# Another finish for the last row block: mean and deviation as six rows, the root taken from the variance, five stores

## The chip, the cores and the metric

The kernel runs on one core of a Trainium2 chip. The metric is the device time of one execution in microseconds. Times of whole executions come from unprofiled runs; the profile is of one more execution, with its own time. "Span" is the stretch from the first to the last recorded instruction or transfer of that execution, and all times of the timeline count from the start of the span.

## The reference

A decoder trunk of two layers on one sequence of 512 tokens with 2048 features, in float32. Layer 0 is differential attention, layer 1 forgetting attention over shared keys and values. Each layer ends in a residual sum and a layer norm; the last one is where the change lies:

```python
def layer_norm(x, g, b):
    xf = x.astype(jnp.float32)
    mu = jnp.mean(xf, axis=-1, keepdims=True)
    var = jnp.mean(jnp.square(xf - mu), axis=-1, keepdims=True)
    y = (xf - mu) * lax.rsqrt(var + EPS)
    return (y * g.astype(jnp.float32) + b.astype(jnp.float32)).astype(x.dtype)
...
        x = layer_norm(DN_ALPHA * x + gate[:, None] * y, ln_g[l], ln_b[l])
```

Here `y` is the output projection of the attention, a product of 512 x 2048 by 2048 x 2048.

## The kernel before, in words

All large products are made in a split form: each float32 operand is split into a rounded part `hi` (type float32r, which TensorE takes in one pass) and the rest `lo`, and three products are summed (`products`, lines 208 to 210). ScalarE makes `hi` (lines 108, 113), VectorE `lo` (lines 109, 114).

The last stage is `out_projection(oB, 1, ...)` (line 1188, called at 1784). It takes the 2048 output columns in four groups f of 512, and the 512 tokens in four row blocks b of 128 partitions. For f = 0, 1, 2 VectorE multiplies the product by the gate, adds the scaled residual, puts the sum into the tile `z` (128 partitions, 4 blocks, 2048 columns) and takes statistics of the 512 columns (line 1243). For f = 3 the accumulators in PSUM start out filled with the residual and the gate is multiplied into the weights beforehand (line 104), so that the sum is ready when the last product ends. In that group the blocks are finished one after the other: six of the eight weight pieces are kept on chip (`held`), TensorE runs all of them for block 0, then for block 1, and so on. When a block's last product is done, `evac` takes the statistics of its last 512 columns (line 1234) and calls `norm_b(b, acc)` (line 1727).

`norm_b` of blocks 0 to 2 aggregates the statistics into mean and variance (`mv`, line 1733), adds EPS (1735), takes the root on ScalarE (1736), centres and multiplies by the gain (`centre`, 1741), forms the reciprocal root with one refining step (`root`, 1744 to 1746), multiplies by it and adds the bias (`finish`, 1750) and stores two halves (1751). While VectorE does that, TensorE multiplies for the next block.

Block 3 has nothing behind it, so its norm is split between engines. For the first 768 columns the formula is written as rstd * (z*g - mean*g + sqrt(var+EPS)*b). The product z*g is put into two PSUM banks ahead of time by `fold_last` (line 1721), which block 2's `norm_b` calls. The rows g and b of these columns are loaded into the tiles `ends`, two rows each (1723, 1724). When mean and deviation are there, they stand side by side in `ms` (128 x 2, lines 1763 and 1766), are transposed by TensorE (1771) and copied to `rows` by ScalarE (1773), and a product of 2 rows by the 512 or 256 columns of `ends` adds the two missing terms onto each bank (1775). These are plain float32 products. ScalarE then multiplies each bank by rstd (1776) and stores it, one from SyncE's queue, one from its own (1777). VectorE does columns 768 to 2047 in the old way: the last 512 are centred straight out of PSUM before the reciprocal root (1764), 768 to 1535 behind it (1778), and both are finished and stored (1779, 1780). Six products on a constant tile (`warm`, 1769) keep TensorE busy between the last product and the transpose.

What sets the order: the program is traced in the order of the code, then a planner with a model of the engines gives every engine its instructions in an order of its own, the traced order counting as priority, and places the waits. An instruction whose inputs are ready early may so be put far ahead of its place in the code. `keep(...)` pins an instruction behind the one traced before it on its engine. Only the start of the kernel has orders written out by hand. Small tiles of 512 columns come from a pool of 16 buffers (`kpool`, through `ktile`), of which weight pieces, residual rows and gates take their share in the last stage. Eight PSUM banks are held as four `acc`, two `sc`, one `tr` and one `o`.

Of the kernel before, what the change touches and what calls it, by code (L numbers as in the profile page):

```python
# [10 lines left out]
F32 = mybir.dt.float32  # L11
F32R = mybir.dt.float32r
I32 = mybir.dt.int32
AF = mybir.ActivationFunctionType
ALU = mybir.AluOpType

P = 128
D = 2048
KT = D // P
T = 512  # L20
# [4 lines left out]
EPS = 1e-5  # L25
# [119 lines left out]
def tile_yoco(  # L145
# [23 lines left out]
    nc = tc.nc  # L169
    V, S, PE, G = nc.vector, nc.scalar, nc.tensor, nc.gpsimd  # L170
# [3 lines left out]
    out = out[0]  # L174
    a_w_in, a_w_out, b_w_in, b_w_out = a_w_in[0], a_w_out[0], b_w_in[0], b_w_out[0]

    const = ctx.enter_context(tc.tile_pool(name="const", bufs=1))
    hpool = ctx.enter_context(tc.tile_pool(name="hpool", bufs=32))
    kpool = ctx.enter_context(tc.tile_pool(name="kpool", bufs=16))
# [10 lines left out]
    def acc_bank(name="acc"):  # L190
        return ps.tile([P, 512], F32, name=name, tag="acc", bufs=4)

    def sc_bank(name="sc"):
        return ps.tile([P, 512], F32, name=name, tag="sc", bufs=2)

    def tr_bank(name="tr"):
        return ps.tile([P, 512], F32, name=name, tag="tr", bufs=1)
# [14 lines left out]
    def corner(sc, q, k):  # L212
# [6 lines left out]
    ident = const.tile([P, P], F32, name="ident")  # L219
    make_identity(nc, ident)  # L220
    ones = const.tile([P, P], F32, name="ones")
    G.memset(ones, 1.0)
    mask = const.tile([P, 512], F32, name="mask")
    G.memset(mask, 0.0)
    G.affine_select(
        out=mask[:, 384:], in_=mask[:, 384:], compare_op=ALU.is_ge, fill=NEG, base=0, pattern=[[-1, P]],
# [13 lines left out]
    pt = tr_bank()  # L240
# [7 lines left out]
    pt = tr_bank()  # L248
# [10 lines left out]
    rows = {}  # L259
# [227 lines left out]
    with tc.tile_pool(name="start", bufs=2, reuse_waits="tile") as sp, tc.manual_schedule(engines=MANUAL):  # L487
# [50 lines left out]
        mtile, xts, acc2, pms, pxs, tmps, split_h, bank = {}, {}, {}, {}, {}, {}, {}, {}  # L538
# [283 lines left out]
    for dst, src, col, bias, one in (  # L822
# [3 lines left out]
        n = len(one)  # L826
# [242 lines left out]
    raw = {}  # L1069

    def keep(key, acc):
        raw[key] = kpool.tile([P, T], F32, name="raw", tag="K")
        S.copy(raw[key], acc)
# [98 lines left out]
    def ktile(name):  # L1172
        return kpool.tile([P, T], F32, name=name, tag="K")
# [197 lines left out]
    npool, n, nstats = zp  # L1371
# [75 lines left out]
    acc = [acc_bank() for _ in range(TB)]  # L1447
# [184 lines left out]
    def attention_pair(p):  # L1632
        sa, ra, da, ta, na, va = attention_b(2 * p)
        sb, rb, db, tb, nb, vb = attention_b(2 * p + 1)
        if p == 7:

            return [
                None, None, sa[0], sa[1], ra[0], [sa[2], ra[1]], da[0], [sa[3], da[1]], [ra[2], ta[0]], [sb[0], ta[1]],
                [ra[3], da[2]], sb[1], [ta[2], da[3]], sb[2], ta[3], va[0], va[1], [nb[0], sb[3]], nb[1], nb[2], None, nb[3], None,
                vb[0], vb[1],  # L1640
            ]
        steps = [
            [], [], [sa[0]], [sa[1]], [ra[0]], [sa[2], ra[1]], [da[0]], [sa[3], da[1]], [ra[2]], [sb[0], ta[0]],
            [ra[3], da[2]], [sb[1], ta[1]], [rb[0], da[3]], [sb[2], ta[2]], [rb[1]], [sb[3], ta[3]],
            [va[0], rb[2]], [va[1]], [db[0], db[1], rb[3]], [db[2]], [tb[0], db[3]], [tb[1]], [tb[2]], [tb[3]], [vb[0]], [vb[1]],
        ]
        return [todo or None for todo in steps]
# [26 lines left out]
    lnrow = {}  # L1674
# [36 lines left out]
        return fn  # L1711

    ahead = {}

    def fold_last():


        pool, z, _ = zp2
        for k, (f0, f1) in enumerate(((0, 512), (512, 768))):
            bank = sc_bank()[:, 0 : f1 - f0]  # L1720
            V.tensor_tensor(bank, z[:, 3, f0:f1], lnrow["g"][:, f0:f1], op=ALU.mult)
            ends = ktile("ends")[0:2, 0 : f1 - f0]
            nc.sync.dma_start(ends[0:1, :], ln_g[1, f0:f1].rearrange("(o n) -> o n", o=1))
            nc.sync.dma_start(ends[1:2, :], ln_b[1, f0:f1].rearrange("(o n) -> o n", o=1))
            ahead[k] = bank, ends, slice(f0, f1)

    def norm_b(b, acc):


        pool, z, stats = zp2  # L1730
        mv = pool.tile([P, 2], F32, name="mv", tag="mv", bufs=4)
        keep = tc.keep_in_program_order
        keep(V.bn_aggr(mv, stats[:, b, :, :]))
        ve, nh, a, rstd = (pool.tile([P, 1], F32, name=k, tag=k, bufs=4) for k in ("lve", "lnh", "lna", "lrstd"))
        keep(V.tensor_scalar(ve, mv[:, 1:2], EPS, None, op0=ALU.add))
        S.activation(rstd, ve, AF.Sqrt)
        keep(V.tensor_scalar(nh, ve, -0.5, None, op0=ALU.mult))

        def centre(f0, f1, src):
            fs = slice(f0, f1)  # L1740
            keep(V.scalar_tensor_tensor(z[:, b, fs], src, mv[:, 0:1], lnrow["g"][:, fs], op0=ALU.subtract, op1=ALU.mult))

        def root():
            keep(V.reciprocal(rstd, rstd))
            keep(V.scalar_tensor_tensor(a, rstd, nh, rstd, op0=ALU.mult, op1=ALU.mult))
            keep(V.scalar_tensor_tensor(rstd, a, 1.5, rstd, op0=ALU.add, op1=ALU.mult))

        def finish(f0, f1):
            fs = slice(f0, f1)
            keep(V.scalar_tensor_tensor(z[:, b, fs], z[:, b, fs], rstd, lnrow["b"][:, fs], op0=ALU.mult, op1=ALU.add))  # L1750
            nc.sync.dma_start(out[b * P : (b + 1) * P, fs], z[:, b, fs])

        if b < 3:
            centre(0, 1536, z[:, b, 0:1536])
            centre(1536, 2048, acc)
            root()
            finish(0, 1024)
            finish(1024, 2048)
            if b == 2:
                fold_last()  # L1760
            return
        ms = pool.tile([P, 2], F32, name="ms", tag="ms")
        keep(V.tensor_scalar(ms[:, 0:1], mv[:, 0:1], -1.0, None, op0=ALU.mult))
        centre(1536, 2048, acc)
        root()
        keep(V.tensor_tensor(ms[:, 1:2], ve, rstd, op=ALU.mult))
        warm = acc_bank("warm")
        for _ in range(6):
            keep(PE.matmul(warm[:, 0:256], mask[:, 0:P], mask[:, 0:256], start=True, stop=True))
        pt = tr_bank()  # L1770
        keep(PE.transpose(pt[0:2, 0:P], ms, ident))
        rows = pool.tile([2, P], F32, name="rows", tag="rows")
        S.copy(rows, pt[0:2, 0:P])
        for (bank, ends, fs), queue in zip(ahead.values(), (nc.sync, nc.scalar)):
            PE.matmul(bank, rows, ends, start=False, stop=True, skip_group_check=True)
            S.activation(z[:, b, fs], bank, AF.Copy, scale=rstd)
            queue.dma_start(out[b * P : (b + 1) * P, fs], z[:, b, fs])
        centre(768, 1536, z[:, b, 768:1536])
        finish(768, 1536)
        finish(1536, 2048)  # L1780

    pieces.extend(attention_pair(7))
    pieces.append(lambda: split_ogb((14, 15)))
    out_projection(oB, 1, zp2, open_z, residual_b, norm_b)
    drain()

# [27 lines left out]
```

## Time and profile before

| what | us |
|---|---|
| median of 3 runs (lowest, highest) | 1928.12 (1927.77, 1928.47) |
| the profiled execution, its own time | 1927.76 |
| its span | 1925.9 |
| TensorE busy in the span | 1911.3 |
| end of the last product of the projection | 1915.81 |
| first store of block 3 issued | 1920.66 |
| last store of block 3 issued | 1921.62 |

A line of the timeline gives start, duration, engine (PE is TensorE, PEld its weight loads, DVE VectorE, ACT ScalarE, POOL GpSimd; SPq and ACTq are DMA issues of SyncE and ScalarE), line of the code, operation, the tiles out<-in with their shapes, and how many instructions it stands for. In square brackets stands how long the engine was idle before it and what ended the wait. A line of the windows gives a stretch of the span, its length, the busy time of each engine, the granted TensorE clock, the busy share of the 16 DMA engines and GB/s. A line of the groups gives busy us, the mean duration of one in ns, and the idle time before.

### The profile page before, as it was taken

What the parts mean: (1) busy time and instruction counts of PE and PEld (TensorE: products, weight loads), DVE (VectorE), ACT (ScalarE), POOL (GpSimd) and SP (SyncE); (2) the same over time, 40 slices, a digit from 0 to 9 for tenths busy, and PEclk for the clock granted to TensorE, in tenths of its full rate; (3) what the DMA queues carried; (4) which work ended last, traced back from release to release, by engine and by line L of the source; (5) the groups of instructions that cost most, each with busy time, mean ns of one, the idle gap of its engine ahead of it and who ended that gap; (6) DMA issues with size and microseconds to landing.
All of it is one profiled execution on the core that took longest, in us unless ns stands there. A gap on an engine that the chain in (4) does not pass through costs nothing.

```text
span 1925.9 us, 25859 instructions
## 1 busy us (share of the span) xinstructions
PE 1911.3 (99%) x8924; PEld 1593.4 (83%) x8924; DVE 1369.5 (71%) x2611; ACT 731.3 (38%) x1262; POOL 2.2 (0%) x10
## 2 busy tenths in 40 slices
PE   8999999999999999999999999999999999999998
PEld 6888888888888888888888898888888888888887
DVE  7994588777676868667675477787566666686767
ACT  3656344333332344521272232224344444453121
POOL 0000000000000000000000000000000000000000
PEclk9999999999999999999999999999999999999999
DMA  9993566676767676476547586785355555555622
GB/s 341 385 336 91 160 186 196 209 239 191 233 199 226 204 222 182 122 241 216 187 165 255 180 296 208 247 272 160 114 150 154 161 150 158 154 153 175 222 90 110
DMA packets 352103, 382.20 MB, mean 198 GB/s; under 512 B 77882, under 2 KB 256082, under 8 KB 351204
## 3 DMA queue, kind: packets, MB, share of 16 engines
q1 hardware_dynamic: 348948, 376.23, 62.1%
q10 hardware_dynamic: 3024, 4.33, 0.6%
q8 instruction: 70, 1.15, 0.2%
q14 instruction: 61, 0.50, 0.1%
HBM read 348.65 MB, written 31.80 MB: 198 GB/s over the span
## 4 chain that ended last, share of the span: by engine, by line
PE 96%; DVE 2%; DMA 1%; SPq 1%; issue 0%; ACT 0%; DVEq 0%; ACTq 0%
PE acc L208 26%; PE acc L209 26%; PE acc L210 26%; PE acc L720 4%; PE sc L720 2%; PE sc L210 1%; PE sc L209 1%; PE sc L208 1%; PE o L208 1%; PE o L210 1%; PE o L209 1%; PE o L720 1%; DMA sms<-in_w_mod_dram 0%; SPq L568 0%; PE tr L686 0%
## 5 line engine op out<-in xcount | busy, mean ns | idle before, releaser
L113 ACT CAST whi<-wst 128x1024 fp32r<-128x1024 f32 (+2 forms) x298 | 303.3, 1018 | 616.4 <-PE acc L210 323.5
L114 DVE TENSOR_TENSOR wlo<-wst,whi 128x1024 fp32r<-128x1024 f32 (+2 forms) x298 | 351.6, 1180 | 241.2 <-ACT whi L113 221.4
L208 PE MATMUL acc<-hh,whi 128*128 128x512 f32 x1184 | 462.9, 391 | 0.0
L209 PE MATMUL acc<-hl,whi 128*128 128x512 f32 x1184 | 461.6, 390 | 0.0
L210 PE MATMUL acc<-hh,wlo 128*128 128x512 f32 x1184 | 460.1, 390 | 0.0
L208 PE MATMUL acc<-whi,hh 128*128 128x512 f32 (+1 forms) x1104 | 418.5, 379 | 0.0
L209 PE MATMUL acc<-wlo,hh 128*128 128x512 f32 (+1 forms) x1104 | 416.7, 377 | 0.0
L210 PE MATMUL acc<-whi,hl 128*128 128x512 f32 (+1 forms) x1104 | 416.2, 377 | 0.0
L433 DVE SCALAR_TENSOR_TENSOR macc<-ms,cact,macc 128x512 f32<-128x512 f32 x307 | 229.3, 747 | 69.9 <-DMA ms<-in_w_mod_dram 51.6
L210 PEld LDWEIGHTS acc<-hh,wlo 128*128 128x128 f32 x1184 | 222.3, 188 | 47.5
L208 PEld LDWEIGHTS acc<-hh,whi 128*128 128x128 f32 x1184 | 222.4, 188 | 44.0 <-DVE sgb L1509 0.8
L209 PEld LDWEIGHTS acc<-hl,whi 128*128 128x128 f32 x1184 | 222.5, 188 | 42.3
L210 PEld LDWEIGHTS acc<-whi,hl 128*128 128x128 f32 x1104 | 207.2, 188 | 38.7
L208 PEld LDWEIGHTS acc<-whi,hh 128*128 128x128 f32 x1104 | 207.3, 188 | 37.4 <-DVE ztmp L1241 0.6
L209 PEld LDWEIGHTS acc<-wlo,hh 128*128 128x128 f32 x1104 | 207.4, 188 | 36.0
L618 DVE SCALAR_TENSOR_TENSOR sacc<-sms,cact,sacc 128x512 f32<-128x512 f32 (+1 forms) x128 | 89.9, 703 | 6.2 <-DMA sms<-in_w_mod_dram 2.8
L904 ACT ACTIVATE e<-e,mn 128x128 f32<-128x128 f32 (+3 forms) x64 | 36.0, 563 | 109.1 <-DVE mn L900 102.5
L1559 ACT ACTIVATE eb<-eb,mnb 128x128 f32<-128x128 f32 (+1 forms) x64 | 35.9, 561 | 72.9 <-DVE mnb L1556 72.5
L720 PE MATMUL acc<-wlo,hh 128*128 128x512 f32 x128 | 49.9, 399 | 0.6 <-DVE wlo L132 0.6
L720 PE MATMUL acc<-whi,hl 128*128 128x512 f32 x128 | 49.4, 393 | 0.0
L720 PE MATMUL acc<-whi,hh 128*128 128x512 f32 x128 | 49.2, 393 | 0.0
L132 DVE TENSOR_TENSOR wlo<-wst,whi 128x768 fp32r<-128x768 f32 (+1 forms) x32 | 34.8, 1088 | 16.9 <-ACT whi L125 12.4
(321 smaller groups left out, 2093.9 us busy)
## 6 DMA issues: line engine op xcount, KB each, us to landing
wst<-in_a_w_in_dram SPq DMA_DIRECT2D x240, 256.0 KB, 3.9
ms<-in_w_mod_dram SPq DMA_DIRECT2D x136, 256.0 KB, 3.9
ms<-in_kv_w_mod_dram SPq DMA_DIRECT2D x64, 512.0 KB, 4.6
wst<-in_b_w_in_dram SPq DMA_DIRECT2D x128, 256.0 KB, 3.0
sms<-in_w_mod_dram SPq DMA_DIRECT2D x56, 512.0 KB, 7.4
wst<-in_kv_w_dram SPq DMA_DIRECT2D x56, 512.0 KB, 4.3
ms<-in_w_mod_dram SPq DMA_DIRECT2D x32, 512.0 KB, 5.1
wst<-in_a_w_out_dram SPq DMA_DIRECT2D x32, 512.0 KB, 4.7
```

Source lines behind the costliest of these rows:

```text
L113: self.nc.scalar.copy(hi[:, :, :w], st[:, :, :w])
L114: self.nc.vector.tensor_tensor(lo[:, :, :w], st[:, :, :w], hi[:, :, :w].bitcast(F32), op=ALU.subtract)
L132: self.nc.vector.tensor_tensor(lo[:, :, :w], st[:, :, :w], hi[:, :, :w].bitcast(F32), op=ALU.subtract)
L208: PE.matmul(dst, lhs[0], rhs[0], start=start, stop=False, skip_group_check=True)
L209: PE.matmul(dst, lhs[0], rhs[1], start=False, stop=False, skip_group_check=True)
L210: PE.matmul(dst, lhs[1], rhs[0], start=False, stop=stop, skip_group_check=True)
L433: ins = V.scalar_tensor_tensor(acc, w, cact[:, kt : kt + 1], acc, op0=ALU.mult, op1=ALU.add)
L618: V.scalar_tensor_tensor(acc, w, sc, acc, op0=ALU.mult, op1=ALU.add)
L720: PE.matmul(bank[n, bk], l, r, start=start, stop=stop, skip_group_check=True)
L904: S.activation(e[:, :w], e[:, :w], AF.Exp, bias=mn, scale=-1.0, accum_out=rs)
L1559: S.activation(e[:, :w], e[:, :w], AF.Exp, bias=mn, scale=-1.0, accum_out=rs)
```

## The change

Only block 3's norm, its preparation and one constant are changed.

The columns that go through PSUM grow from 768 to 1280, in three chunks of 512, 512 and 256; the third takes a bank of `acc`. They are prepared by the call for block 1 instead of block 2. Mean and deviation are each split into a rounded part and a rest, and g and b as well: the product has 6 rows (high mean and deviation with the high and the low parts of g and b, low mean and deviation with the high parts) and float32r operands. For that `ends_of` loads g and b into three pairs of rows, copies them on ScalarE (which rounds) and subtracts on VectorE to leave the low part in the first pair.

The root of block 3 is half the deviation, taken by ScalarE from the variance itself, with scale 0.25 and a constant tile `qeps` (0.25 * EPS, filled by GpSimd at the start) as bias. The deviation comes from it by one step of Newton, ahead of the reciprocal root, which gets its own step afterwards. The last 512 columns are centred behind the transpose. Five warming products are left of six. VectorE keeps columns 1280 to 2047. The five stores of the block are pinned in the order: chunk 0, columns 1536 to 2047, chunk 1 (all SyncE), chunk 2 (ScalarE's queue), columns 1280 to 1535 (SyncE).

```diff
--- before.py
+++ after.py
@@ -220,6 +220,8 @@
     make_identity(nc, ident)
     ones = const.tile([P, P], F32, name="ones")
     G.memset(ones, 1.0)
+    qeps = const.tile([P, 1], F32, name="qeps")
+    G.memset(qeps, 0.25 * EPS)
     mask = const.tile([P, 512], F32, name="mask")
     G.memset(mask, 0.0)
     G.affine_select(
@@ -1711,18 +1713,27 @@
         return fn
 
     ahead = {}
-
-    def fold_last():
-
-
+    CHUNKS = ((0, 512), (512, 1024), (1024, 1280))
+
+    def ends_of(f0, f1):
+
+
+        w = f1 - f0
+        raw = ktile("raw")[0:6, 0:w]
+        for k, src in enumerate((ln_g, ln_b)):
+            nc.sync.dma_start(raw[k:6:2, :], src[1, f0:f1].partition_broadcast(3))
+        ends = kpool.tile([P, T], F32R, name="ends", tag="K")[0:6, 0:w]
+        S.copy(ends, raw)
+        V.tensor_tensor(ends[0:2, :], raw[0:2, :], ends[0:2, :].bitcast(F32), op=ALU.subtract)
+        return ends
+
+    def fold_last(banks):
         pool, z, _ = zp2
-        for k, (f0, f1) in enumerate(((0, 512), (512, 768))):
-            bank = sc_bank()[:, 0 : f1 - f0]
-            V.tensor_tensor(bank, z[:, 3, f0:f1], lnrow["g"][:, f0:f1], op=ALU.mult)
-            ends = ktile("ends")[0:2, 0 : f1 - f0]
-            nc.sync.dma_start(ends[0:1, :], ln_g[1, f0:f1].rearrange("(o n) -> o n", o=1))
-            nc.sync.dma_start(ends[1:2, :], ln_b[1, f0:f1].rearrange("(o n) -> o n", o=1))
-            ahead[k] = bank, ends, slice(f0, f1)
+        for k, bank in banks:
+            fs = slice(*CHUNKS[k])
+            bank = bank()[:, 0 : fs.stop - fs.start]
+            V.tensor_tensor(bank, z[:, 3, fs], lnrow["g"][:, fs], op=ALU.mult)
+            ahead[k] = bank, ends_of(*CHUNKS[k]), fs
 
     def norm_b(b, acc):
 
@@ -1732,52 +1743,69 @@
         keep = tc.keep_in_program_order
         keep(V.bn_aggr(mv, stats[:, b, :, :]))
         ve, nh, a, rstd = (pool.tile([P, 1], F32, name=k, tag=k, bufs=4) for k in ("lve", "lnh", "lna", "lrstd"))
-        keep(V.tensor_scalar(ve, mv[:, 1:2], EPS, None, op0=ALU.add))
-        S.activation(rstd, ve, AF.Sqrt)
-        keep(V.tensor_scalar(nh, ve, -0.5, None, op0=ALU.mult))
 
         def centre(f0, f1, src):
             fs = slice(f0, f1)
             keep(V.scalar_tensor_tensor(z[:, b, fs], src, mv[:, 0:1], lnrow["g"][:, fs], op0=ALU.subtract, op1=ALU.mult))
 
-        def root():
+        def finish(f0, f1):
+            fs = slice(f0, f1)
+            keep(V.scalar_tensor_tensor(z[:, b, fs], z[:, b, fs], rstd, lnrow["b"][:, fs], op0=ALU.mult, op1=ALU.add))
+            store = nc.sync.dma_start(out[b * P : (b + 1) * P, fs], z[:, b, fs])
+            if b == 3:
+                keep(store)
+
+        if b < 3:
+            keep(V.tensor_scalar(ve, mv[:, 1:2], EPS, None, op0=ALU.add))
+            S.activation(rstd, ve, AF.Sqrt)
+            keep(V.tensor_scalar(nh, ve, -0.5, None, op0=ALU.mult))
+            centre(0, 1536, z[:, b, 0:1536])
+            centre(1536, 2048, acc)
             keep(V.reciprocal(rstd, rstd))
             keep(V.scalar_tensor_tensor(a, rstd, nh, rstd, op0=ALU.mult, op1=ALU.mult))
             keep(V.scalar_tensor_tensor(rstd, a, 1.5, rstd, op0=ALU.add, op1=ALU.mult))
-
-        def finish(f0, f1):
-            fs = slice(f0, f1)
-            keep(V.scalar_tensor_tensor(z[:, b, fs], z[:, b, fs], rstd, lnrow["b"][:, fs], op0=ALU.mult, op1=ALU.add))
-            nc.sync.dma_start(out[b * P : (b + 1) * P, fs], z[:, b, fs])
-
-        if b < 3:
-            centre(0, 1536, z[:, b, 0:1536])
-            centre(1536, 2048, acc)
-            root()
             finish(0, 1024)
             finish(1024, 2048)
-            if b == 2:
-                fold_last()
+            if b == 1:
+                fold_last(((0, sc_bank), (1, sc_bank), (2, acc_bank)))
             return
-        ms = pool.tile([P, 2], F32, name="ms", tag="ms")
-        keep(V.tensor_scalar(ms[:, 0:1], mv[:, 0:1], -1.0, None, op0=ALU.mult))
-        centre(1536, 2048, acc)
-        root()
-        keep(V.tensor_tensor(ms[:, 1:2], ve, rstd, op=ALU.mult))
+
+
+        half, inv = (pool.tile([P, 1], F32, name=k, tag=k) for k in ("half", "inv"))
+        S.activation(half, mv[:, 1:2], AF.Sqrt, scale=0.25, bias=qeps)
+        ms = pool.tile([P, 1, 2], F32, name="ms", tag="ms")
+        keep(V.tensor_scalar(ve, mv[:, 1:2], EPS, 0.25, op0=ALU.add, op1=ALU.mult))
+        keep(V.tensor_scalar(ms[:, 0, 0:1], mv[:, 0:1], -1.0, None, op0=ALU.mult))
+        keep(V.reciprocal(inv, half))
+        keep(V.scalar_tensor_tensor(ms[:, 0, 1:2], inv, ve, half, op0=ALU.mult, op1=ALU.add))
+        six = pool.tile([P, 3, 2], F32R, name="six", tag="six")
+        keep(V.tensor_copy(six[:, 0:2, :], ms.to_broadcast([P, 2, 2])))
+        keep(V.tensor_tensor(six[:, 2:3, :], ms, six[:, 0:1, :].bitcast(F32), op=ALU.subtract))
+        keep(V.tensor_scalar(nh, ve, -0.25, None, op0=ALU.mult))
+        keep(V.scalar_tensor_tensor(a, inv, nh, inv, op0=ALU.mult, op1=ALU.mult))
+        keep(V.scalar_tensor_tensor(rstd, a, 0.75, inv, op0=ALU.add, op1=ALU.mult))
         warm = acc_bank("warm")
-        for _ in range(6):
+        for _ in range(5):
             keep(PE.matmul(warm[:, 0:256], mask[:, 0:P], mask[:, 0:256], start=True, stop=True))
         pt = tr_bank()
-        keep(PE.transpose(pt[0:2, 0:P], ms, ident))
-        rows = pool.tile([2, P], F32, name="rows", tag="rows")
-        S.copy(rows, pt[0:2, 0:P])
-        for (bank, ends, fs), queue in zip(ahead.values(), (nc.sync, nc.scalar)):
+        keep(PE.transpose(pt[0:6, 0:P], six.bitcast(F32).rearrange("p u k -> p (u k)"), ident))
+        rows = pool.tile([6, P], F32R, name="rows", tag="rows")
+        S.copy(rows, pt[0:6, 0:P])
+        for bank, ends, _ in ahead.values():
             PE.matmul(bank, rows, ends, start=False, stop=True, skip_group_check=True)
-            S.activation(z[:, b, fs], bank, AF.Copy, scale=rstd)
-            queue.dma_start(out[b * P : (b + 1) * P, fs], z[:, b, fs])
-        centre(768, 1536, z[:, b, 768:1536])
-        finish(768, 1536)
+
+        def scaled(k, queue):
+            bank, _, fs = ahead[k]
+            keep(S.activation(z[:, b, fs], bank, AF.Copy, scale=rstd))
+            keep(queue.dma_start(out[b * P : (b + 1) * P, fs], z[:, b, fs]))
+
+        scaled(0, nc.sync)
+        centre(1536, 2048, acc)
         finish(1536, 2048)
+        scaled(1, nc.sync)
+        scaled(2, nc.scalar)
+        centre(1280, 1536, z[:, b, 1280:1536])
+        finish(1280, 1536)
 
     pieces.extend(attention_pair(7))
     pieces.append(lambda: split_ogb((14, 15)))
```

## The prediction

> **What bounds the kernel now.** I read the busy shares and the chain that ended last on the page first, then the timeline of the last 11 us, because the change touches little before them.
>
> ```profile
> PE 1911.3 (99%) x8924; PEld 1593.4 (83%) x8924; DVE 1369.5 (71%) x2611; ACT 731.3 (38%) x1262; POOL 2.2 (0%) x10
> PE 96%; DVE 2%; DMA 1%; SPq 1%; issue 0%; ACT 0%; DVEq 0%; ACTq 0%
> ```
>
> TensorE is busy for 99% of the span and is 96% of the chain. The matrix products are not touched, so the change can win only in what follows the last of them. That tail, in order of time (start, duration, engine, line):
>
> ```profile
> 1915.64 2.75 PE L1769 MATMUL warm<-mask 128*128 128x256 f32 x12
> 1915.85 0.70 DVE L1234 BATCH_NORM_STATS2 zstats<-acc 128x6 f32<-128x512 f32 x1 [1.36 <-PE acc L210]
> 1916.58 0.27 DVE L1733 BATCH_NORM_AGGREGATE mv<-zstats 128x2 f32<-128x24 f32 x1
> 1916.88 0.15 DVE L1735 TENSOR_SCALAR lve<-mv 128x1 f32<-128x1 f32 x1
> 1917.07 0.20 ACT L1736 ACTIVATE lrstd<-lve 128x1 f32<-128x1 f32 x1 [7.96 <-DVE lve L1735]
> ...
> 1917.86 0.15 DVE L1744 RECIPROCAL lrstd<-lrstd 128x1 f32<-128x1 f32 x1
> 1918.05 0.22 DVE L1745 SCALAR_TENSOR_TENSOR lna<-lrstd,lnh 128x1 f32<-128x1 f32 x1
> 1918.30 0.16 DVE L1746 SCALAR_TENSOR_TENSOR lrstd<-lna,lrstd 128x1 f32<-128x1 f32 x1
> 1918.49 0.16 DVE L1766 TENSOR_TENSOR ms<-lve,lrstd 128x1 f32<-128x1 f32 x1
> 1918.57 1.01 DVE L1741 SCALAR_TENSOR_TENSOR z<-z,mv,ln_g 128x768 f32<-128x768 f32 x1
> ...
> 1918.71 0.27 PE L1771 MATMUL tr<-ident,ms 128*2 128x128 f32 x1 [0.31 <-DVE ms L1766]
> 1919.02 0.26 ACT L1773 COPY rows<-tr 2x128 f32<-2x128 f32 x1 [1.75 <-PE tr L1771]
> ...
> 1919.33 1.55 PE L1775 MATMUL sc<-ends,rows 2*128 2x512 f32 x4 [0.34 <-ACT rows L1773]
> 1919.62 1.68 DVE L1750 SCALAR_TENSOR_TENSOR z<-z,lrstd,ln_b 128x768 f32<-128x768 f32 x2
> ```
>
> ```profile
> 1920.48 0.69 ACT L1776 ACTIVATE z<-sc,lrstd 128x512 f32<-128x512 f32 x1 [1.21 <-PE sc L1775]
> ```
>
> ```profile
> 1920.66 0.33 SPq L1751 DMA_DIRECT2D out_dram<-z  x1
> 1921.20 0.33 SPq L1777 DMA_DIRECT2D out_dram<-z  x1
> 1921.57 0.40 ACTq L1777 DMA_DIRECT2D out_dram<-z  x1
> 1921.62 0.41 SPq L1751 DMA_DIRECT2D out_dram<-z  x1
> ```
>
> Statistics, root, then two-row products on one side and elementwise work on the other; the first store is issued at 1920.66. After it the stretches of the span (the last two columns are the share of the DMA engines and GB/s) decide:
>
> ```profile
> 1921.00:1921.50 0.50, 0.00 (x0) 0.00 (x0) 0.30 (x1) 0.50 (x2) 0.00 (x0) 1.00 0.01 6
> 1921.50:1922.00 0.50, 0.00 (x0) 0.00 (x0) 0.00 (x0) 0.04 (x1) 0.00 (x0) 1.00 1.06 430
> ...
> 1923.50:1924.00 0.50, 0.00 (x0) 0.00 (x0) 0.00 (x0) 0.00 (x0) 0.00 (x0) 0.50 1.07 408
> 1924.00:1924.50 0.50, 0.00 (x0) 0.00 (x0) 0.00 (x0) 0.00 (x0) 0.00 (x0) 0.50 0.27 98
> ```
>
> The DMA engines are idle until 1921.5 and full from then on; the last half microsecond has 0.27 of a stretch, so they finish at about 1924.2. The 1 MB of block 3 is thus one unbroken stream of 2.7 us, which starts 0.84 us after the first issue (1921.50 - 1920.66). From its end to the end of the span (1925.9) pass another 1.7 us that hold no work of the kernel. So **the end is the issue of the first store + 0.84 + 2.7 + 1.7**, as long as the later stores arrive before the stream runs dry.
>
> **The change part by part.** Durations and distances are those of the rows above unless a row is added. A dependent small VectorE instruction starts 0.19 us after the one before (1917.86 to 1918.05), 0.25 after a three-operand one (1918.05 to 1918.30); an independent one after 0.08 (1918.49 to 1918.57); another engine answers about 0.04 after the end.
>
> *Root.* ScalarE now reads the variance itself, with 0.25 and a tile as scale and bias, so it starts at 1916.88 where the addition of EPS stood, 0.19 earlier. Its price with a tile as operand is not in the trace; the nearest rows are three ScalarE instructions of 512 columns with no, one and two operands from a tile: 0.62 and 0.77 here, 0.69 above.
>
> ```profile
> 1869.81 0.62 ACT L108 CAST held<-wst 128x512 fp32r<-128x512 f32 x1 [1.83 <-DVE wst L104]
> ```
>
> ```profile
> 14.85 0.77 ACT L694 ACTIVATE hh<-px,mcol 128x512 fp32r<-128x512 f32 x1
> ```
>
> So an operand from a tile costs up to 0.08, and the root between 0.20 and 0.28; I take 0.28, since it is one added operand of that kind. It ends at 1917.16. [...]
>
> *To the transpose.* Reciprocal at 1917.19, the half-step that gives the deviation +0.19 at 1917.38, the copy into two parts +0.25 at 1917.63, the subtraction of the rest +0.19 at 1917.82, end (+0.16) 1917.98. None of these shapes (128x4) stands in the trace; the small rows run from 0.15 to 0.22, so two added instructions are worth 0.30 to 0.50 and I hold 0.35. What goes in exchange is the centring of 512 columns (0.66 before the reciprocal) and the third and fourth instruction of the root, which now run behind the subtraction. The transpose starts at 1918.04 instead of 1918.71. Five warming products instead of six, at 2.75 / 12 = 0.23 per pass, free TensorE at about 1917.95, just before; a sixth would have held it until 1918.4.
>
> *Products.* The copy of the rows starts at 1918.35 and the first product at 1918.65. Before, one bank of 512 columns took two f32 passes, from 1919.33 until ScalarE began at 1920.48: 1.15 us. Now it is one pass with rounded operands. The first such pass of this kernel after a pause:
>
> ```profile
> 15.67 0.73 PE L720 MATMUL sc<-hh,whi 128*128 128x512 f32 x2
> ```
>
> Two take 0.73, and the second follows 0.23 behind, so one from a standstill takes 0.50. That row uses 128 rows and ours 6, so the bounds are 0.4 and the old 1.15; I take 0.50. ScalarE scales bank 0 from 1919.18 to 1919.87 and its store is issued at **1919.90**. The factor is there by then: its last instruction starts at 1918.34.
>
> *The later stores.* The remaining durations, by shape (fifth and sixth numbers: busy us, mean ns):
>
> ```profile
> L1750 DVE SCALAR_TENSOR_TENSOR z<-z,lrstd,ln_b 128x512 f32<-128x512 f32 x1 | 0.7, 746 | 0.0
> L1741 DVE SCALAR_TENSOR_TENSOR z<-acc,mv,ln_g 128x512 f32<-128x512 f32 x1 | 0.7, 743 | 0.0
> ...
> L1776 ACT ACTIVATE z<-sc,lrstd 128x256 f32<-128x256 f32 x1 | 0.5, 467 | 0.0
> ```
>
> VectorE centres the last 512 columns at 1918.42 and finishes them at 1919.95. SyncE takes 0.42 from one issue to the next (1921.20 to 1921.62), so that store goes at 1920.32, bank 1 (scaled by 1920.46) at 1920.74, bank 2 on ScalarE's queue at 1920.87, the last 256 columns at 1921.16. Each store's data could begin 0.84 later, at 1921.16, 1921.58, 1921.71 and 2.00 past 1920; the stream needs them at about 1921.4, 1922.1, 1922.7 and 1923.1. It never runs dry. A pinned SyncE queue adds waits of one store for the one ahead; behind them stand only stores. A fifth store adds some hundredths, so I take 2.8 for the stream: 1920.74 + 2.8 = 1923.55 against 1924.2, and a span of 1925.2. [...]
>
> *Preparation.* Moved from block 2 to block 1 and enlarged: VectorE gets 256 more columns in bank 1, bank 2, and three subtractions; ScalarE three copies; SyncE six small loads for four. The rows around it:
>
> ```profile
> 1886.44 1.23 DVE L114 TENSOR_TENSOR wlo<-wst,whi 128x1024 fp32r<-128x1024 f32 x1
> ...
> 1888.18 0.69 DVE L1721 TENSOR_TENSOR sc<-z,ln_g 128x512 f32<-128x512 f32 x1
> ...
> 1889.38 0.43 DVE L1721 TENSOR_TENSOR sc<-z,ln_g 128x256 f32<-128x256 f32 x1
> ...
> 1891.36 0.70 DVE L1234 BATCH_NORM_STATS2 zstats<-acc 128x6 f32<-128x512 f32 x1 [0.95 <-PE acc L210]
> ```
>
> VectorE's addition is 0.26 + 0.43 + 0.69 + 0.69 + 0.43 = 2.5 us. It has 0.95 us of idle time ahead of block 0's statistics and 1.36 ahead of block 3's; blocks 1 and 2 run the same instructions at the same distance and so have about 1.36 each: 5.0 in all. I cost it at nothing; without that cover it would cost what is left over. ScalarE waits 7.96 us before the last root, and SyncE's loads have no store behind them until block 0 ends.
>
> *The constant.* One more fill on GpSimd at the start. The first product waits for a load, not for GpSimd, and that stays:
>
> ```profile
> 2.55 0.26 PE L241 MATMUL tr<-ident,crow 16*128 16x16 f32 x1 [2.55 <-DMA crow<-in_c_dram]
> ```
>
> **Sum.** First issue 0.76 earlier, stream 0.06 longer: 0.70 us. The profiled execution took 1927.76 (span 1925.9); the median of the three runs is 1928.12, 0.36 above it. 1927.76 - 0.70 = 1927.06, and on the median's footing **1927.4**. That is 0.04%: less than 0.2%, about what a measurement of this kernel can tell from no change.
>
> **Rivals.** *The tail gives less (0.13).* If the product with 6 rows still takes 1.15, the first store is issued at 1920.55 and 0.1 remains: 1928.0. If not the stream but the last issue sets the end at a constant distance, 1921.62 to 1921.16 leaves 0.46: 1927.7. For it speaks that no row shows a 6-row product; against it the idle DMA engines until 1921.5.
>
> *Preparation comes into the weights' way (0.11), and the kernel is slower.* The order on VectorE and ScalarE is planned, and a copy or a subtraction may be put ahead of the last split of weights, where it waits for its small load. The split ends at 1887.67 and TensorE first reads it here:
>
> ```profile
> 1889.80 0.19 PEld L209 LDWEIGHTS acc<-wlo,hh 128*128 128x128 f32 x1
> ```
>
> ```profile
> wst<-in_b_w_in_dram SPq DMA_DIRECT2D x128, 256.0 KB, 3.0
> ```
>
> From 2.1 us of delay on (1889.8 - 1887.67), TensorE stalls, and from 2.8 on the kernel is slower than before. All of the added 2.5 us ahead of the split, and up to the 3.0 us that a load takes to land (above), make a stall of 0.4 to 3.4; less the 0.7 won, 1927.8 to 1930.8, in the middle 1929.3. Against it: the same kind of work was put at 1888.18, behind the split.
>
> *The plan of the whole kernel comes out differently (0.06)*, from the added constant or the enlarged pools: an order written for one state of the buffers meets another. Price unknown, say 4 us or more, in either direction, more likely slower; nothing in the profile speaks for it.
>
> **How the numbers follow.** The forecast has 0.70, with 1926.8 to 1927.9 as its own range (root 0.20, product 0.40 and the small instructions give 0.2 more, the fifth store and slower ones 0.2 less; the runs scatter by 0.35). The lesser gain reaches 1928.1 and two fifths of the second rival 1929.0: 0.70 + 0.13 + 0.04 = 0.87 between 1926.5 and 1929.0. Beyond 0.2% (under 1924.3 or over 1932.0) lies only the third rival: 0.02 faster, 0.04 slower, 0.94 within.
>
> **What would show it.** Right: the root at 1916.88 directly behind the aggregation, the transpose near 1918.0, one record per bank of about 0.4 to 0.5, the first store near 1919.9 and a stream without a gap that ends near 1923.5. Wrong: block 3's statistics later than 0.04 behind the last product, a TensorE wait for wlo near 1889.8, a gap in the stream, or a distance from stream to end other than 1.7.

## The result and the profile after

The changed kernel takes **1936.43 us** (median of 6 runs, 1935.25 to 1938.09) against 1928.06 for the kernel before (6 runs, 1927.61 to 1928.83). The ratio is 1.0043, with a 95% interval of 1.0030 to 1.0056. That is 8.4 us slower, where 0.7 us faster was forecast, and outside the range. The profiled execution has a span of 1934.7 us.

Two rows split the difference. The first is the last product of the projection in the timeline of the kernel after:

```profile
1924.87 0.40 PE L210 MATMUL acc<-whi,hl 128*128 128x512 f32 x1
```

It ends at 1925.27; before it ended at 1915.81. So **9.46 us are lost ahead of the tail**. From there to the end of the span pass 1934.70 - 1925.27 = 9.43 us, against 1925.94 - 1915.81 = 10.13: **the tail won the 0.70 that was forecast.**

The second pair is one and the same copy of a weight piece on ScalarE, early in the kernel, before and after:

```profile
141.84 1.05 ACT L125 CAST whi<-wst 128x1024 fp32r<-128x1024 f32 x1
```

```profile
150.95 1.05 ACT L125 CAST whi<-wst 128x1024 fp32r<-128x1024 f32 x1
```

The copy takes 1.05 us in both, and it is 9.11 us late by then. Nearly all of the loss lies in the first 150 us, 1.7 ms away from anything the change was about. There the kernel waits for loads, as the stretches of the span show, first before and then after (TensorE's busy us and products, the other engines, clock, DMA share, GB/s):

```profile
0.00:150.00 150.00, 141.64 (x674) 117.48 (x675) 130.02 (x193) 79.68 (x120) 2.16 (x10) 1.00 1.01 344
50.00:100.00 50.00, 50.00 (x246) 41.76 (x245) 45.54 (x64) 31.57 (x48) 0.00 (x0) 1.00 1.09 385
```

```profile
0.00:150.00 150.00, 135.84 (x630) 110.22 (x631) 122.48 (x182) 71.56 (x106) 1.64 (x10) 1.00 1.08 334
50.00:100.00 50.00, 47.66 (x227) 38.64 (x225) 43.63 (x60) 29.39 (x45) 0.00 (x0) 1.00 1.09 349
```

Read the last two columns of the second rows together. The DMA engines are as full as before (1.09), but they move 349 GB/s instead of 385. They do not wait more; each packet takes longer. The packet records of the first 130 us (one for each piece that a DMA engine moved, with its size and duration) say the same: a packet of 1024 bytes took 46.7 ns on the mean before and 51.5 after, one of 512 bytes 27.2 and 30.6, one of 2048 bytes 84.2 and 89.5. TensorE, full in that stretch before, has gaps now. The view of waits in the first 150 us (total us, times, longest) names who waits, before and then after (line 618 of the kernel before is 620 of the kernel after):

```profile
ACT whi L125 <- DMA wst<-in_a_w_in_dram: 22.1, 6, 10.4
DVE sacc L618 <- DMA sms<-in_w_mod_dram: 2.8, 4, 1.3
```

```profile
ACT whi L125 <- DMA wst<-in_a_w_in_dram: 37.7, 16, 12.0
DVE sacc L620 <- DMA sms<-in_w_mod_dram: 8.8, 11, 2.6
```

The chain that ended last shows it too. TensorE's share falls from 96% to 91%, and DMA's rises from 1% to 4%:

```profile
PE 1913.7 (99%) x8921; PEld 1592.9 (82%) x8921; DVE 1371.2 (71%) x2617; ACT 733.7 (38%) x1266; POOL 2.2 (0%) x11
PE 91%; DMA 4%; DVE 3%; SPq 1%; ACT 1%; issue 1%; DVEq 0%; ACTq 0%
```

What in the change reaches back to the start? Apart from the fill of `qeps`, every engine has the same instructions in the same order as before until the preparation in the last stage. The difference that is left is in the memory plan of the built program. The new tile of 4 bytes per partition takes a slot of 32 bytes ahead of all working pools, and so **every later buffer stands 32 bytes higher**: `sms`, which the loads of the start fill, at 160032 instead of 160000, `wst` at 119072 instead of 119040, `xt` at 200992 instead of 200960. The old addresses are multiples of 256 bytes, and so are the distances between the buffers of a pool.

### The profile page after: what moved, and what is told of

Its sections match the earlier page's. It is cut to its first block, busy times and chain, and to the rows that moved or that the text cites. A ratio compares the mean times of both kernels' runs of the same rounds, so it can differ in the third digit from the quotient of the medians.

```text
span 1934.7 us, 25873 instructions
## 1 busy us (share of the span) xinstructions
PE 1913.7 (99%) x8921; PEld 1592.9 (82%) x8921; DVE 1371.2 (71%) x2617; ACT 733.7 (38%) x1266; POOL 2.2 (0%) x11
## 3 DMA queue, kind: packets, MB, share of 16 engines
q8 instruction: 70, 1.15, 0.2%
## 4 chain that ended last, share of the span: by engine, by line
PE 91%; DMA 4%; DVE 3%; SPq 1%; ACT 1%; issue 1%; DVEq 0%; ACTq 0%
PE acc L208 26%; PE acc L209 26%; PE acc L210 26%; PE acc L722 2%; DMA sms<-in_w_mod_dram 1%; PE sc L210 1%; PE sc L209 1%; PE sc L208 1%; PE o L208 1%; PE o L210 1%; PE o L209 1%; DMA wst<-in_a_w_in_dram 1%; PE sc L722 1%; DMA xt<-in_x_dram 1%; DVE sacc L620 1%; SPq L570 1%
## 5 line engine op out<-in xcount | busy, mean ns | idle before, releaser
L125 ACT CAST whi<-wst 128x768 fp32r<-128x768 f32 (+1 forms) x32 | 30.2, 943 | 58.9 <-DMA wst<-in_a_w_in_dram 37.7
```

Source lines behind the costliest of these rows:

```text
L125: self.nc.scalar.copy(hi[:, :, :w], self.stage[self.done][:, :, :w])
```

## The experiments

**Theory A**: the loss comes from the addresses of the loads' destinations alone. A1 says that a boundary of 64 bytes is enough for the old speed, A2 that it takes a wider one. Rival B looks for the loss not in the addresses but in what the change adds, rival C in another chip or moment with slower memory.

### The kernel before with all buffers 32 or 64 bytes higher

```diff
-    pcol = const.tile([P, 38], F32, name="pcol")
+    pcol = const.tile([P, 46], F32, name="pcol")
...
-        V.tensor_copy(pcol, pt[:, 0:38])
+        V.tensor_copy(pcol[:, 0:38], pt[:, 0:38])
```

The second kernel has `[P, 54]`. Nothing of the change is in either; a constant tile is wider, and its added columns are not used.

> The kernel before with one edit: the constant tile pcol is made 8 columns wider, so that every buffer laid out after it (all work pools) stands 32 bytes higher in the on-chip memory; the instructions and their order stay as they were. The changed kernel lost 9.4 us before its last product ended (1925.27 against 1915.81 in the span), nearly all of it in the first 150 us, and its 1024-byte load packets took 51 to 54 ns there instead of 46. Theory A (addresses: the new constant takes 32 bytes ahead of all pools, and loads into buffers that no longer start on their old boundary are slower): about 1937.5, 9.4 over the kernel before, with the longer packets. Rival B (the new fill on GpSimd or the new work of the tail does it, not the addresses): 1928.1, as before. Rival C (another chip or another moment with slower memory): 1928.1, and the kernel before beside it the same.

> As the first run, with pcol 16 columns wider, so that everything behind it stands 64 bytes higher. It tells apart which boundary counts, if addresses count. In the kernel before, the buffers of the start's loads stand on multiples of 256 bytes; here they stand on multiples of 64 and not of 128. Theory A1 (64 bytes count): 1928.1, as before, and 1024-byte packets of 46 ns. Theory A2 (256 bytes count, or any move is bad): slow, 1935 to 1940. [...] Rival B (not the addresses): 1928.1, and then the first run is at 1928.1 as well.

The first took 1937.2 us against 1927.6 (ratio 1.0049, 1.0036 to 1.0061), the second 1936.58 (1.0046, 1.0033 to 1.0060). The stretch from 50 to 100 us of the first:

```profile
50.00:100.00 50.00, 47.00 (x224) 38.16 (x222) 43.04 (x59) 29.41 (x45) 0.00 (x0) 1.00 1.09 350
```

350 GB/s at a DMA share of 1.09, as in the kernel after. A shift of 32 bytes makes the whole loss without any of the change, with the kernel before at 1927.6 beside it, so A stands and the rivals fall; 64 bytes are no better, so A1 falls.

### The change with the old addresses, and with 64 bytes

```diff
-    qeps = const.tile([P, 1], F32, name="qeps")
-    G.memset(qeps, 0.25 * EPS)
...
-    neglam = const.tile([P, 1], F32, name="neglam")
+    both = const.tile([P, 2], F32, name="neglam")
+    neglam, qeps = both[:, 0:1], both[:, 1:2]
+    G.memset(qeps, 0.25 * EPS)
```

Here `qeps` lives in the unused part of the 32-byte slot of another constant, so that no later buffer moves. The second kernel instead makes the tile of `qeps` 64 bytes wide (`[P, 16]`, first column used).

> The changed kernel, with its constant put into the second column of a constant tile that has a single column and 32 bytes of room, so that no buffer moves against the kernel before. The whole tail, the fill on GpSimd and the earlier preparation stay as changed. Theory A: the start is as before, and only the tail's 0.67 us (10.11 to 9.43 us from the end of the last product to the end of the span) remain: 1927.4. Rival B: 1936.4, as the changed kernel.

> The changed kernel with its constant 16 columns wide (64 bytes instead of 32), so that all buffers behind it stand 64 bytes higher than in the kernel before. Theory A1 (64-byte boundaries count): 1927.4, as the third run. Theory A2 (256-byte boundaries, or any move): 1935 to 1940. Rival B: 1936.4.

With the old addresses the change took **1926.9 us** against 1927.6 (11 and 15 runs; ratio 0.9997, 0.9988 to 1.0005); with 64 bytes it took 1935.61 (1.0044, 1.0032 to 1.0057). The first is the lowest median of any version with the change, but its interval holds 1: it can't be told from the kernel before. Its start and its tail:

```profile
50.00:100.00 50.00, 50.00 (x245) 41.69 (x245) 45.45 (x64) 32.35 (x49) 0.00 (x0) 1.00 1.09 385
```

```profile
1915.92 0.40 PE L210 MATMUL acc<-whi,hl 128*128 128x512 f32 x1
...
1919.20 0.72 PE L1795 MATMUL sc<-ends,rows 6*128 6x512 f32 x2 [0.34 <-ACT rows L1793]
1919.73 1.27 ACT L1799 ACTIVATE z<-sc,lrstd 128x512 f32<-128x512 f32 x2 [0.58 <-DVE z L1749]
...
1920.44 0.33 SPq L1800 DMA_DIRECT2D out_dram<-z  x1
```

385 GB/s are back, the first store is issued 1920.44 - 1916.32 = 4.12 us after the last product (4.85 before), and the span ends 9.3 us after it (10.1 before).

### How wide the boundary is

The kernel before once more, with `pcol` as `[P, 70]` (+128 bytes) and `[P, 102]` (+256 bytes).

> Everything behind pcol 128 bytes higher: load buffers on multiples of 128, not of 256. If 256-byte boundaries count: slow, 1936 to 1937. If 128-byte boundaries count: 1927.6. [...]

> As the first run, with everything behind pcol 256 bytes higher, so that the load buffers of the start stand on multiples of 256 again. Theory A2 with 256-byte boundaries: 1927.6, as the kernel before, and 1024-byte packets of 46 ns. Theory A3 (any other place than the old one is bad, or the amount moved counts): 1936 to 1937, as with 32 and 64.

At +128 it took 1936.51 against 1927.47 (1.0045, 1.0030 to 1.0060), at +256 1927.8 (1.0001, 0.9992 to 1.0011). The stretch from 50 to 100 us of the two:

```profile
50.00:100.00 50.00, 47.68 (x228) 38.60 (x227) 43.69 (x60) 29.93 (x46) 0.00 (x0) 1.00 1.10 350
```

```profile
50.00:100.00 50.00, 50.00 (x246) 41.74 (x245) 45.55 (x65) 32.23 (x49) 0.00 (x0) 1.00 1.09 385
```

Moving the buffers as such costs nothing (+256: 1927.8). Off a 256-byte boundary the loads are slow, and equally so at 32, 64 and 128 bytes: at each of the three that stretch has 350 GB/s instead of 385, and the whole time is 9.6, 9.0 and 9.0 us above the kernel before. The mean packet of 1024 bytes rose alike too, from 46.7 ns before to 51.5 in the kernel after (+32) and to 51.8 at +128.

### Which buffers: two attempts

At first the two groups of buffers were shifted by longer weight tiles, 4128 bytes each instead of 4096: `wlo` alone, which moves `sms` and `xt` by 96 bytes, and `pcol` at +64 with `whi` and `wlo`, which leaves the weights' buffers off the boundary and puts `sms` and `xt` back on it.

```diff
-        lo = self.pool.tile([P, 2, 512], F32R, name="wlo", tag="wlo", bufs=3)
+        lo = self.pool.tile([P, 1032], F32R, name="wlo", tag="wlo", bufs=3)[:, 0:1024].rearrange("p (k n) -> p k n", k=2)
...
```

(The same edit stands in the second place where the tile is made; in the second attempt `whi` has it too.)

> The kernel before, with each of the three wlo tiles 32 bytes longer: the weight buffers (wst) keep their addresses on multiples of 256, and only what is laid out behind wlo, the pool with the modulation weights (sms) and x, stands 96 bytes off. Theory A2 with each load paying for its own place: of the packets of the first 130 us, sms and x hold about two thirds of the bytes, so some 6 of the 9.4 us: 1933 to 1935. Rival (the loss comes from the weights alone): 1927.6. Rival (one buffer off slows all): 1937.

> The kernel before, with pcol 64 bytes and each whi and wlo tile 32 bytes longer: now the weight buffers (wst) and the small tiles of the pool ahead of them stand 64 bytes off, and the pool with sms and x is 256 bytes higher, on multiples of 256. Theory A2 with each load paying for its own place: about 3 of the 9.4 us, 1930 to 1932. Rival (the modulation weights alone): 1927.6. Rival (one buffer off slows all): 1937.

They took 1951.15 (1.0120, 1.0103 to 1.0137) and 1957.63 (1.0154, 1.0138 to 1.0169), far from all that was expected. Neither loses much at the start: TensorE is busy for 141.05 and 141.82 of the first 150 us, against 141.64 in the kernel before. The loss goes on through the whole kernel; a stretch in its middle, of the kernel before and of the second attempt:

```profile
500.00:700.00 200.00, 200.00 (x922) 166.88 (x921) 149.68 (x304) 72.30 (x133) 0.00 (x0) 1.00 0.70 213
```

```profile
500.00:700.00 200.00, 200.00 (x906) 164.11 (x905) 145.22 (x295) 70.10 (x128) 0.00 (x0) 1.00 0.69 212
```

TensorE is as full and its clock the same, but it does 906 products instead of 922. The longer tiles seem to have brought a cost of their own, so these two runs decide nothing about loads. The shift was made again without touching the weights' tiles, by a spare tile behind them in their pool, of 128 bytes (below), or of 192 (`[P, 48]`) with `pcol` at +64:

```diff
+        spare = wpool.tile([P, 32], F32, name="spare", tag="spare", bufs=1)
+        G.memset(spare, 0.0)
```

> The question of the seventh run again, without longer whi and wlo tiles, since both runs with them (1951, 1958) had slower products in the whole kernel: a spare tile of 128 bytes at the end of the weights' pool moves only what lies behind it, sms and x among it, 128 bytes up; whi, wlo and wst stay where they were. If the longer tiles were what slowed the products: the products are as before, and only the start loses, by its packets in the seventh run (1024 bytes: 48.3 ns against 46.7 before and 51.5 with all off) a third of the 9.4 us: 1929 to 1932. If an odd distance between buffers slowed the products: about 1950 again.

> The question of the eighth run without longer tiles: pcol 64 bytes longer, so that the weight buffers stand 64 bytes off, and a spare tile of 192 bytes behind them, so that sms and x are 256 bytes up, on multiples of 256 again. If the longer tiles slowed the products, they are as before here; the packets of the eighth run were as before (46.8 ns), so the start loses little: 1927.6 to 1929. If each load pays for its own place: 1930 to 1932. If an odd distance between buffers slowed the products: 1950 or more.

The start's buffers alone cost 3.6 us (1931.42 against 1927.8; 1.0020, 1.0010 to 1.0029), inside the 1929 to 1932 that their packets had let expect; the weights' alone cost nothing (1926.72; 0.9994, 0.9985 to 1.0003). The stretches of the two:

```profile
50.00:100.00 50.00, 50.00 (x245) 41.81 (x244) 45.58 (x64) 33.12 (x51) 0.00 (x0) 1.00 1.09 372
500.00:700.00 200.00, 200.00 (x920) 166.83 (x919) 149.50 (x303) 72.64 (x134) 0.00 (x0) 1.00 0.71 215
```

```profile
50.00:100.00 50.00, 50.00 (x245) 41.84 (x244) 45.60 (x64) 31.42 (x48) 0.00 (x0) 1.00 1.09 384
500.00:700.00 200.00, 200.00 (x923) 167.05 (x922) 149.95 (x305) 72.19 (x133) 0.00 (x0) 1.00 0.71 218
```

The products in the middle are at the old rate again (920 and 923 in 200 us), so it was the longer tiles that slowed them. But 3.6 + 0 is not the 9 us of both together, and that sum **stays open**. The packet records say a little more. Of the 1024-byte packets in the first 130 us of the span, these took 46 or 47 ns:

| kernel | such packets | of |
|---|---|---|
| before | 35,909 | 36,154 |
| weights' buffers off | 35,690 | 36,271 |
| start's buffers off | 25,977 | 36,011 |
| after | 9,361 | 33,822 |

The weights' loads use packets of that size too, and with their buffers alone off the boundary they are as quick as ever: 98% of all took 46 or 47 ns, against 99% before. With the start's buffers off it was 72%, and in the kernel after, with all of them off, it is still 28%. So it is not a fixed price per packet off the boundary; the share of slow packets rose with the share of the traffic that was off. What makes a packet slow, no run here shows.

### The tail by itself

Both kernels start from the change with the old addresses, and each was executed once. One makes the six-row product in plain float32 (`ends`, `six` and `rows` as F32, so that the low parts become zero), the other leaves out the store of chunk 2, so that 256 columns of block 3 stay unwritten.

```diff
-        ends = kpool.tile([P, T], F32R, name="ends", tag="K")[0:6, 0:w]
+        ends = kpool.tile([P, T], F32, name="ends", tag="K")[0:6, 0:w]
...
-        six = pool.tile([P, 3, 2], F32R, name="six", tag="six")
+        six = pool.tile([P, 3, 2], F32, name="six", tag="six")
...
-        rows = pool.tile([6, P], F32R, name="rows", tag="rows")
+        rows = pool.tile([6, P], F32, name="rows", tag="rows")
```

```diff
-            keep(queue.dma_start(out[b * P : (b + 1) * P, fs], z[:, b, fs]))
+            if k < 2:
+                keep(queue.dma_start(out[b * P : (b + 1) * P, fs], z[:, b, fs]))
```

> The third run (the change at the old addresses) with plain float32 for the six rows, their columns and the product; the copies and subtractions stay, the low parts become zero. My theory of the tail (first store = end of bank 0's product + scaling, then one unbroken stream): the product of bank 0 takes 1.1 us instead of 0.5, the first issue comes 0.6 us later behind the last product of the projection (4.12 us in the third run, so 4.7), and so does the end, 0.5 to 0.6 us. Rival (the last 512 columns on VectorE, not the product, set when scaling can begin, as the profile names them): no change of the first issue.

> The third run with the store of the third chunk (128 KB on ScalarE's queue) left out; its columns of the result are missing. Theory (the stream of data sets the end): the stream is shorter by those bytes, 0.35 us, and the span behind the last product of the projection is 0.3 to 0.4 us shorter. Rival (the last issue sets the end): no change, since the last store is issued at the same moment.

The float32 product, in the timeline:

```profile
1918.74 0.74 DVE L1749 SCALAR_TENSOR_TENSOR z<-acc,mv,ln_g 128x512 f32<-128x512 f32 x1
...
1918.98 1.98 PE L1795 MATMUL sc<-ends,rows 6*128 6x512 f32 x4 [0.34 <-ACT rows L1793]
...
1920.14 0.69 ACT L1799 ACTIVATE z<-sc,lrstd 128x512 f32<-128x512 f32 x1 [1.21 <-PE sc L1795]
...
1920.85 0.33 SPq L1800 DMA_DIRECT2D out_dram<-z  x1
```

ScalarE begins 1.16 us behind the start of the product, where the rounded form takes 0.53 (1919.20 to 1919.73 above). The last product of this execution ends at 1916.10, so the first store is issued 4.75 behind it instead of 4.12: **one pass instead of two is worth 0.63 us.** The rival of this run, that VectorE's centring of the last 512 columns sets when scaling can begin, falls: the centring had ended at 1919.48, 0.66 ahead of the scaling. The span ends 10.07 behind the last product, 0.75 later. (The whole time was 1927.95.) The end follows the first issue, as the prediction had it, and by a little more than the same amount.

Without chunk 2's store the kernel took 1926.93. The last product ends at 1916.13, the first and the last store are issued at the same distances behind it as with five stores:

```profile
1920.25 0.33 SPq L1801 DMA_DIRECT2D out_dram<-z  x1
...
1921.65 0.41 SPq L1754 DMA_DIRECT2D out_dram<-z  x1
```

Yet the span ends 9.03 behind it instead of 9.32. If the last issue set the end, nothing would have been won; 0.29 us went with an eighth of the bytes, of which the stream's 2.8 us would give 0.35. By its packets the stream was 2.53 us long instead of 2.83. That speaks for the stream, though this is one execution.

How far such a distance can be trusted: from the last product to the end passed 10.12 to 10.16 us in all nine profiled executions with the old tail, and 9.43 in both of the change off the boundary.

## Why the prediction was wrong

**The step that failed** is *the constant*: "One more fill on GpSimd at the start. The first product waits for a load, not for GpSimd, and that stays". It priced the instruction and left out the storage. The instruction is indeed free, as the timeline of the kernel after shows:

```profile
1.35 0.10 POOL L224 MEMSET qeps<- 128x1 f32 x1
...
2.41 0.25 PE L243 MATMUL tr<-ident,crow 16*128 16x16 f32 x1 [2.41 <-POOL mask L227]
```

The fill takes 0.10 us, and the first product starts no later than before (2.55). It does wait for GpSimd's `mask` now, not for the load, but that cost nothing. The 32 bytes that the tile occupies cost 9 us, which the shift alone repeats (1937.2) and the old addresses alone remove (1926.9).

**The rival of another plan** (0.06) named "the added constant or the enlarged pools" and "say 4 us or more", and had the right culprit with the wrong mechanism: the order of the instructions did not change ahead of the last stage. Memory was not weighed as a resource with a position at all, although the load-bound start was there to be seen.

**The tail came out as worked up to the first store.** Set back by 9.46 us, the times of after stand beside the forecast: root at 1916.88 (1916.88), transpose 1918.07 (1918.04), product 1918.69 (1918.65), first store 1919.94 (1919.90), last store 1921.33 (1921.16). The rows themselves:

```profile
1926.34 0.29 ACT L1775 ACTIVATE half<-mv,qeps 128x1 f32<-128x1 f32 x1 [7.78 <-DVE mv L1744]
1926.66 0.16 DVE L1779 RECIPROCAL inv<-half 128x1 f32<-128x1 f32 x1
1926.86 0.22 DVE L1780 SCALAR_TENSOR_TENSOR ms<-inv,lve,half 128x1 f32<-128x1 f32 x1
1927.11 0.17 DVE L1782 CAST six<-ms 128x4 fp32r<-128x4 f32 x1
1927.32 0.16 DVE L1783 TENSOR_TENSOR six<-ms,six 128x2 fp32r<-128x2 f32 x1
...
1927.53 0.27 PE L1791 MATMUL tr<-ident,six 128*6 128x128 f32 x1
...
1927.91 0.74 DVE L1749 SCALAR_TENSOR_TENSOR z<-acc,mv,ln_g 128x512 f32<-128x512 f32 x1
1928.15 0.72 PE L1795 MATMUL sc<-ends,rows 6*128 6x512 f32 x2 [0.34 <-ACT rows L1793]
...
1928.68 1.27 ACT L1799 ACTIVATE z<-sc,lrstd 128x512 f32<-128x512 f32 x2 [0.58 <-DVE z L1749]
...
1929.40 0.33 SPq L1800 DMA_DIRECT2D out_dram<-z  x1
...
1930.79 0.41 SPq L1754 DMA_DIRECT2D out_dram<-z  x1
```

- *Root*: 0.29, where 0.28 was taken. *One pass per bank*: ScalarE starts 0.53 behind the start of the product, as worked (1918.65 to 1919.18). By its own record the first pass took 0.49. VectorE's centring ends at 1928.65, within 0.01 of it, and the profile names the centring; which of the two releases ScalarE here is not shown, so a shorter product alone might bring nothing more.
- *The stream*: by its packets it begins 0.83 behind the first issue, as before, and never runs dry, but lasts longer than the 2.8 of the forecast. In the full stretches of the tail it is 338 to 377 GB/s. The forecast showed 430 and 408 of the kernel before, but those between them ran lower, down to the first row here (before); the other rows are of the kernel after:

```profile
1922.00:1922.50 0.50, 0.00 (x0) 0.00 (x0) 0.00 (x0) 0.00 (x0) 0.00 (x0) 1.00 0.96 379
```

```profile
1930.00:1930.50 0.50, 0.00 (x0) 0.00 (x0) 0.35 (x1) 0.31 (x1) 0.00 (x0) 1.00 0.52 201
1930.50:1931.00 0.50, 0.00 (x0) 0.00 (x0) 0.00 (x0) 0.00 (x0) 0.00 (x0) 1.00 1.00 373
...
1932.50:1933.00 0.50, 0.00 (x0) 0.00 (x0) 0.00 (x0) 0.00 (x0) 0.00 (x0) 0.50 0.99 338
1933.00:1933.50 0.50, 0.00 (x0) 0.00 (x0) 0.00 (x0) 0.00 (x0) 0.00 (x0) 0.50 0.20 68
```

  By its packets it took 2.98 us (2.75 before). Here `z`, which it reads, is off the boundary too; with the old addresses it took 2.83. What lies between stream and end was 1.5 instead of 1.7 in both, which the forecast had named as a sign of being wrong. The two errors cancel. They do so in the five profiled executions of the old tail with `z` off the boundary too: there the stream took 2.89 to 2.91 us and the rest 1.55 to 1.57, and the span ended 5.29 to 5.30 behind the first issue, against 5.27 to 5.29 in the four with `z` on it. So a stream that is slower off the boundary does not move the end, and the fixed 1.7 of the working does not hold; why is not shown. The 0.70 came out by some luck: the end kept its distance from the first issue (5.31 after), though the terms in between were not those of the working.
- *Preparation*: costed at nothing, and block 3's statistics start 0.04 behind the last product as before. The cover was used as described: block 0's statistics do not wait for their product at all, block 1's only 0.35, those of block 3 the full 1.37. The second rival, a stall ahead of the weights, did not come: TensorE has no wait in the view of waits from 1890 to 1925.
- *The lesser gain*: with the old addresses the tail won 0.8 us, and the scaling begins 0.53 behind the product, not 1.15. Its other form, an end at a fixed distance from the last issue, gives 0.29 for the kernel after (5.52 behind the last product instead of 5.81), where 0.70 was won. That rival is refuted. The whole time moved by 0.7 of 1927.6, inside its interval, as "no change" had it.

## What to carry to other kernels

Before adding a constant or widening a tile, ask what stands behind it in memory: where a stage is bound by loads, look whether the destinations of its loads stand on multiples of 256 bytes; here they ran at 385 GB/s on such multiples and at 350 off them, and a 4-byte tile placed ahead of them cost 9 us, where the change it served won 0.7 in the tail. The sign here was a loss far from the edited lines, with the DMA engines equally full (1.09) and fewer GB/s; shifting the kernel before by one slot of 32 bytes (1937.2 us), and putting the change back on the old addresses (1926.9), told it apart in two runs.

## What the runs showed of the hardware

- Loads whose destinations all stand 32, 64 or 128 bytes off a 256-byte boundary ran at 350 GB/s instead of 385 while the DMA engines were full (a share of 1.09 to 1.10), and the cost was nearly the same for the three distances (9.6, 9.0 and 9.0 us). With only the start's buffers off it was 372 GB/s (3.6 us), with only the weights' 384 (no cost). Why these don't add up is open.
- Weight tiles of 4128 bytes instead of 4096 slowed the products of the whole kernel: 906 instead of 922 in 200 us at a full clock where both `whi` and `wlo` were longer, 911 where `wlo` alone was. The two runs took 24 and 30 us more in all; some 4 of the 24 belong to the start's buffers, by the run that moved them alone. The distance from the boundary is not the reason: with tiles of 4096 bytes it was 923 with the weights 64 bytes off, and 921 with everything 32 bytes off. Whether the length itself or the distance from tile to tile does it is not shown.
